# A two-layer hybrid decoder trunk on one core: the order of all instructions from a list scheduler over the recorded program

## The chip, the core and the metric

One core of one Trainium2 chip runs the whole kernel as one program. The metric is device microseconds of an execution; the kernel before has a median of 1129.89 us over 3 runs. Engines are called as in the profile: PE (TensorE matmul), PEld (its weight load), DVE (VectorE), ACT (ScalarE), POOL (GpSimd), SP (SyncE, which issues most loads).

## The reference, cut to what matters

256 tokens of width 1024 pass two layers. In each, three branches mix tokens from the same normalized input: NSA sparse attention, an RWKV-7 recurrence and an S5 diagonal state-space model; a sigmoid gate per channel merges them. Cross-attention to 256 memory tokens and a SwiGLU feed-forward of width 2816 follow. Each sub-layer normalizes its input and its output (RMSNorm).

```python
def layer(x, p):
    h = rmsnorm(x, p.g0)
    z = h @ w_in          # nsa q | k, v (x3) | gates | rwkv | s5 | 3 merge gates of 1024
    y = sum(sigmoid(g_b) * (branch_b(z_b) @ up_b) for b in (nsa, rwkv, s5))
    x = x + rmsnorm(y @ w_merge_out, p.g1)
    x = x + rmsnorm(cross_attention(rmsnorm(x, p.g2), mem), p.g3)
    x = x + rmsnorm(swiglu(rmsnorm(x, p.g4)), p.g5)
```

All of it is fp32.

## The kernel before, in words

Tokens lie in two tiles of 128 rows, x[0] and x[1] (xt in the code), which stay in SBUF. PE multiplies fp32 operands as sums of products of a high and a low part (hi, lo): one main product is three matmuls, high by high, high by low, low by high (mm3, lines L349 to L351). Weights come in 264 units of 128 x 1024 (class Weights): SP loads a unit into one of 3 raw buffers (L315), ACT copies it to its high part wh (L298), and raw minus wh gives the low part wl (L299, in split). This subtraction is done by DVE or POOL in turns that the table ENGS names by stage (W.engs); up to 3 units are ready ahead, and the last TAIL = 2 have buffers of their own.

The main products of a layer run in one stream (mixer_main): q, k and v of NSA, the inputs of RWKV and S5, the merge gates, the products of the branches' outputs (up) and their merge. The branches (rwkv, s5, nsa) are streams of small products, transposes and elementwise work. A stream yields where its next product waits for other engines, and drive steps through the streams by a string, MIX, with one letter a step (m main, r, s, n). S5 treats 8 blocks j of states per layer; each ends with four products into a strip of 32 columns of one bank (L925 to L928), after its scans (L916, L917) and POOL's rotations (L919 to L921).

After the mixer come the merge-out product and a chain that is the same after each sub-layer: Post.half squares and scales a half of a tile's result from PSUM (L444 to L447), Post.end takes 1 / rms by Newton steps on one number per token (rsqrt, L366 to L381) and adds to x (L458); NormT.tile then transposes x (L294) and writes its high and low parts (ACT L416, DVE L417), with which the next products begin. So each token tile passes one such chain between two sub-layers. At the boundary of the layers the last LAST = 4 units of tile 1's feed-forward are held back (finish) and stand behind the first steps of layer 1's q.

The order on each engine is the tile framework's: it takes the program order that streams and drive give, and reorders by its own timeline, with priority to NormT.tile, Post.half and Post.end (decorator first, HPX = 30).

```python
with tile.TileContext(nc, schedule_with_timeline_sim=True) as tc:
    body(tc, t)
```

## Time and profile before

| | before |
|---|---|
| runs, us | 1126.42, 1129.89, 1131.2 (median 1129.89) |
| span of the profiled execution, us | 1125.9; the median of the runs is 4.0 above it (no own time of this execution is listed) |
| busy: PE / PEld / DVE / ACT / POOL | 92% / 80% / 68% / 48% / 57% |
| mean granted TensorE clock | 0.963 |
| moved by DMA | 161.52 MB, mean 143 GB/s |

Busy is a share of the span. Matmuls are pipelined, so a busy PE may still be slower than its pace; the clock says how much of full speed was granted. By stage: start 0 to 28 us, layer 0's mixer 28 to 292, merge-out and cross-attention 292 to 386, feed-forward 386 to 548, boundary of the layers 548 to 591, layer 1's mixer 591 to 844, its cross-attention to 945, feed-forward and end to 1126.

### The profile page before, as it was taken

The page shows a single profiled execution, that of the slowest core. Times are in us where ns is not written, and L with a number is a line of the kernel's source. Part 1 is how long each engine was busy: PE and PEld are TensorE (multiplying, and loading weights), DVE is VectorE, ACT ScalarE, POOL GpSimd, SP SyncE. Part 2 cuts the span into 40 slices and gives each one's busy share as a digit, 9 for nine tenths or more (in the row PEclk, how much of TensorE's full clock was granted, in tenths as well). Part 3 has the DMA queues.
Part 4 walks back from the last instruction along what each step waited for, and adds up shares of the span by engine and source line. Part 5 has one row for each costly group of instructions (what it writes and reads, how often), then busy time and mean ns, then how long its engine had stood idle before and what let it go on. Part 6 is the DMA issues. An engine that isn't in the chain of part 4 may idle for free. (4 is left out here: it accounts for less than half of the span.)

```text
span 1125.9 us, 20473 instructions
## 1 busy us (share of the span) xinstructions
PE 1037.2 (92%) x7890; PEld 900.0 (80%) x7890; DVE 763.2 (68%) x1405; ACT 540.1 (48%) x1040; POOL 647.3 (57%) x762
## 2 busy tenths in 40 slices
PE   8887898999987999999888899999999869999997
PEld 7876676788875799998667776889788748999985
DVE  6667699898766646575458698796995764333633
ACT  7523244456555634454345242545565546444542
POOL 6999787533462586910147578964335434655543
PEclk9998999999988999999989899999899889999999
DMA  6530632244541446555434236223245314655552
GB/s 233 205 122 20 224 115 76 76 155 166 180 141 57 152 159 219 186 185 189 142 100 147 67 113 225 76 93 111 84 164 189 130 56 149 203 183 184 181 192 89
DMA packets 43153, 161.52 MB, mean 143 GB/s; under 512 B 5040, under 2 KB 5168, under 8 KB 41776
## 3 DMA queue, kind: packets, MB, share of 16 engines
q1 hardware_dynamic: 41472, 155.45, 40.7%
q10 hardware_dynamic: 1584, 4.77, 1.2%
q8 instruction: 62, 1.02, 0.4%
q14 instruction: 35, 0.29, 0.1%
HBM read 159.15 MB, written 1.05 MB: 142 GB/s over the span
## 5 line engine op out<-in xcount | busy, mean ns | idle before, releaser
L299 POOL TENSOR_TENSOR wl<-raw,wh 128x1024 fp32r<-128x1024 f32 (+1 forms) x123 | 296.7, 2420 | 327.4 <-ACT wh L298 322.0
L298 ACT ACTIVATE wh<-raw 128x1024 fp32r<-128x1024 f32 (+1 forms) x268 | 282.0, 1055 | 254.5 <-PE mm L350 107.4
L349 PE MATMUL mm<-b,wh 128*128 128x256 f32 x1344 | 386.7, 288 | 2.6 <-DVE b L1274 1.3
L351 PE MATMUL mm<-b,wl 128*128 128x256 f32 x1344 | 386.0, 288 | 1.0 <-DVE wl L299 1.0
L350 PE MATMUL mm<-b,wh 128*128 128x256 f32 x1344 | 384.4, 286 | 0.2 <-DVE b L945 0.2
L299 DVE TENSOR_TENSOR wl<-raw,wh 128x1024 fp32r<-128x1024 f32 (+1 forms) x145 | 196.7, 1357 | 166.8 <-ACT wh L298 166.6
L349 PEld LDWEIGHTS mm<-b,wh 128*128 128x128 f32 x1344 | 256.8, 191 | 12.0 <-issue 4.0
L351 PEld LDWEIGHTS mm<-b,wl 128*128 128x128 f32 x1344 | 256.6, 191 | 9.0 <-issue 6.7
L350 PEld LDWEIGHTS mm<-b,wh 128*128 128x128 f32 x1344 | 256.9, 191 | 5.7 <-issue 4.7
L350 PE MATMUL px<-wl,b 128*128 128x512 f32 x248 | 98.0, 399 | 0.0
L349 PE MATMUL px<-wh,b 128*128 128x512 f32 x248 | 97.0, 401 | 1.0 <-ACT b L298 1.0
L351 PE MATMUL px<-wh,b 128*128 128x512 f32 x248 | 97.2, 400 | 0.0
L349 PE MATMUL mm<-wh,b 128*128 128x512 f32 (+2 forms) x192 | 71.8, 382 | 13.0 <-ACT b L416 8.8
L351 PE MATMUL mm<-wh,b 128*128 128x512 f32 (+2 forms) x192 | 68.5, 370 | 5.5 <-DVE b L417 4.7
L350 PE MATMUL mm<-wl,b 128*128 128x512 f32 (+2 forms) x192 | 68.9, 364 | 0.5 <-DVE wl L299 0.5
L294 PE MATMUL px<-ident,b 128*128 128x128 f32 (+2 forms) x280 | 47.3, 287 | 12.8 <-DVE b L1432 6.7
L349 PEld LDWEIGHTS mm<-wh,b 128*128 128x128 f32 x192 | 39.8, 209 | 22.2 <-ACT b L416 13.4
L349 PEld LDWEIGHTS px<-wh,b 128*128 128x128 f32 x248 | 47.3, 191 | 11.9 <-ACT b L298 1.4
L351 PEld LDWEIGHTS px<-wh,b 128*128 128x128 f32 x248 | 47.1, 190 | 11.2
L350 PEld LDWEIGHTS px<-wl,b 128*128 128x128 f32 x248 | 47.2, 190 | 11.0
L416 ACT ACTIVATE b<-px,cols 128x128 fp32r<-128x128 f32 x128 | 41.1, 366 | 30.1 <-DVE b L417 17.2
L1568 POOL TENSOR_TENSOR b<-b,b 128x256 f32<-128x256 f32 x40 | 39.5, 989 | 26.8 <-ACT b L1567 26.7
(348 smaller groups left out, 1735.7 us busy)
## 6 DMA issues: line engine op xcount, KB each, us to landing
raw<-in_w SPq DMA_DIRECT2D x264, 512.0 KB, 3.5
b<-in_w SPq DMA_DIRECT2D x8, 1024.0 KB, 5.2
b<-in_gains ACTq DMA_DIRECT2D x6, 512.0 KB, 4.1
raw<-in_w SPq DMA_DIRECT2D x6, 420.0 KB, 3.1
b<-in_mem SPq DMA_DIRECT2D x4, 512.0 KB, 5.0
mats<-in_mats SPq DMA_DIRECT2D x1, 1152.0 KB, 7.6
mats<-in_mats ACTq DMA_DIRECT2D x1, 1152.0 KB, 6.8
x<-in_x SPq DMA_DIRECT2D x2, 512.0 KB, 5.3
```

Of the source, the lines that this page charges most:

```text
L294: PE.transpose(out, in_, ident[:k, :k])
L298: A.activation(dst_h, src, AF.Copy)
L299: eng.tensor_tensor(dst_l, src, dst_h.bitcast(F), op=OP.subtract)
L349: PE.matmul(out, lh, rh, start=start, stop=False)
L350: PE.matmul(out, lh, rl, start=False, stop=False)
L351: PE.matmul(out, ll, rh, start=False, stop=stop)
L416: A.activation(self.h[:, n, sl], pt[:, kk], AF.Copy, scale=g[:, n:n + 1])
L1568: G.tensor_tensor(s_, s_, tg[:, 1], op=OP.mult)
```

## The change

The body is run once with engines that only record: each call on DVE, POOL, ACT, PE or SP is kept with its stream (w for weights, m, r, s, n in the mixers, M elsewhere), and all tiles get tags and numbers of buffers. A function plan then lays these operations out in time by a model of costs and takes the order on each engine from it; it also chooses between DVE and POOL for elementwise operations of 64 elements a row or more whose operands all lie in SBUF, between DVE and ACT for plain copies, and among the 8 PSUM banks (tile names bank0 to bank7). The body is run again with these banks, and the operations are issued in that order under a manual schedule, from one line, L2171; so every instruction of the changed kernel has this line. The main products (mm3) keep their order among themselves.

```diff
+class Eng:
...
+            elif what in EITHER and on in (("V",), ("G",)):
...
+                if xs and not any(x.tensor.name in r.psum for x in xs) and _count(xs[0].ap[1:]) >= 64:
+                    on = ("V", "G")
+            r.ops.append((on, what, a, k, r.stream, r.chain))
...
+def _locks(op, eng, out, ins, psum):
+    if eng == "G":
+        return op[1] != "memset"
+    if eng != "V" or any(x.tensor.name in psum for x in out + ins):
+        return False
+    if op[1] in ("tensor_copy", "tensor_scalar"):
+        return _count(out[0].ap[1:]) >= 64 or op[1] == "tensor_copy"
+    return len(ins) > 1
...
+def plan(rec, info=None):
...
+        al = ALPHA.get(ops[i][4], 1.0)
...
+        for j, kind in succ[i] + extra.get(i, []):
+            b = max(b, lvl[j] + ((lat + SEM) if kind else occ) * al)
...
+    for q, bonus in BONUS.items():
...
+            lvl[i] += 1000 * bonus[k * len(bonus) // len(js)]
...
+            if info[j]["locks"].get(e):
+                wait = max(wait, shared)
...
+            if e == "PE":
+                sh, cs = info[j]["cells"]
+                if sh == shape:
+                    wait = max([wait] + [cell[x][y] for x, y in cs])
...
[...]
...
+            if sh != shape:
+                now = max([now] + [x for y in cell for x in y]) + SWITCH
```

BONUS holds, for each stream, 24 numbers of us that are added to the priority of its pieces, and ALPHA a factor on the paths of r, s and n (2.0, 2.2, 2.0). The body itself changes in these places:

```diff
-BUFS = {'tiny': 17, 'b1': 10, 'b2': 20, 'b4': 6, 'b8': 4}
+BUFS = {'tiny': 17, 'b1': 9, 'b2': 21, 'b4': 6, 'b8': 4}
...
-TAIL = 2  # last units of weights, which have buffers of their own
+W_SLOTS = {"raw": 3, "wh": 4, "wl": 4}
...
-            yield
-            o = pyy[q, J]
-            PE.matmul(o, CC[:, 0, j], q1[:, 0], start=True, stop=False)
-            PE.matmul(o, CC[:, 1, j], q1[:, 1], start=False, stop=False)
-            PE.matmul(o, CC[:, 2, j], q2[:, 0], start=False, stop=False)
-            PE.matmul(o, CC[:, 2, j], q2[:, 1], start=False, stop=True)
+            qs.append((pyy[q, J], j, q1, q2))
+            if len(qs) == NB:
+                for n, (c_, i) in enumerate(((0, 0), (1, 1), (2, 0), (2, 1))):
+                    for o, j_, q1, q2 in qs:
+                        PE.matmul(o, CC[:, c_, j_], (q1, q2)[n // 2][:, i], start=n == 0, stop=n == 3)
...
-            for qq in range(2):
-                w1 = sb([P, 2048])
+            for qq in range(4):
+                w1 = sb([P, 1024])
...
-            tc.keep_in_program_order(load_mats(0, m))
+            load_mats(0, m)
...
-        W.engs = engs(2 if l else 1)
...
+    with tc.manual_schedule():
+        for i, e in planned[0]:
...
+            getattr(real[e], what)(*a, **k)
```

MIX loses two letters of its first string; ENGS, W.engs and the decorator first have no effect any more. At the boundary, finish() now stands ahead of taking q's four units in the code. In NormT.tile the two banks of a token tile are evicted in turns. On SP the constants (128 x 1830) and mats (128 x 2304) come ahead of the fourth unit of weights; before, both stood behind the tenth.

Three places of the order follow. The chain of main products is interrupted by other matmuls in 177 places before and in 264 now; DVE has 142 low parts (wl) before and 262 now, POOL 120 and 2.

DVE after layer 0's merge-out: Post's last half, the Newton steps on tiny tiles, the addition to x. Before:

```order
L373 TENSOR_SCALAR tiny_813_3948<-tiny_782_3812 128x1
L445 TENSOR_TENSOR b4_784_3814<-px_780_3810,b4_776_3805 128x512
L366 SCALAR_TENSOR_TENSOR tiny_814_3950<-tiny_813_3948,tiny_782_3812 128x1
L447 TENSOR_SCALAR tiny_785_3815<-tiny_785_3815 128x1
L378 SCALAR_TENSOR_TENSOR tiny_815_3952<-tiny_814_3950 128x1
L379 SCALAR_TENSOR_TENSOR tiny_816_3953<-tiny_815_3952,tiny_813_3948 128x1
L366 SCALAR_TENSOR_TENSOR tiny_818_3957<-tiny_816_3953,tiny_782_3812 128x1
L381 SCALAR_TENSOR_TENSOR tiny_817_3954<-tiny_818_3957,tiny_816_3953 128x1
L373 TENSOR_SCALAR tiny_819_3989<-tiny_785_3815 128x1
L458 SCALAR_TENSOR_TENSOR x_2_81<-b4_781_3811,tiny_817_3954,x_2_81 128x512 x2
```

and now:

```order
L2171 TENSOR_SCALAR tiny_630_704<-tiny_599_673 128x1
L2171 SCALAR_TENSOR_TENSOR tiny_631_705<-tiny_630_704,tiny_599_673 128x1
L2171 SCALAR_TENSOR_TENSOR tiny_632_706<-tiny_631_705 128x1
L2171 SCALAR_TENSOR_TENSOR tiny_633_707<-tiny_632_706,tiny_630_704 128x1
L2171 SCALAR_TENSOR_TENSOR tiny_635_709<-tiny_633_707,tiny_599_673 128x1
L2171 TENSOR_TENSOR wl_647_721<-raw_645_719,wh_646_720 128x1024
L2171 SCALAR_TENSOR_TENSOR tiny_634_708<-tiny_635_709,tiny_633_707 128x1
L2171 SCALAR_TENSOR_TENSOR x_1_74<-b4_598_672,tiny_634_708,x_1_74 128x512
L2171 TENSOR_TENSOR wl_650_724<-raw_648_722,wh_649_723 128x1024
L2171 SCALAR_TENSOR_TENSOR x_1_74<-b4_598_672,tiny_634_708,x_1_74 128x512
L2171 TENSOR_TENSOR wl_663_737<-raw_661_735,wh_662_736 128x1024
L2171 SCALAR_TENSOR_TENSOR b8_562_636<-bank7_71,cols_3_77,b8_561_635 128x128
```

The steps of one token tile now stand together, with one wl among them and two around the addition. Before, those of both tiles alternate, and no wl stands among them on DVE; POOL's own order has a row of wl there.

PE at the boundary of the layers. x_2_81 is the first token tile before, x_1_74 now; px_1274 and bank4_68 hold the second half of tile 1's feed-forward. Before:

```order
L349 MATMUL px_1274_6291<-wh_1350_6640,b2_1356_6664 128x512
L350 MATMUL px_1274_6291<-wl_1351_6641,b2_1356_6664 128x512
L351 MATMUL px_1274_6291<-wh_1350_6640,b2_1357_6665 128x512
L349 MATMUL px_1274_6291<-wh_1353_6658,b2_1356_6664 128x512
L350 MATMUL px_1274_6291<-wl_1354_6659,b2_1356_6664 128x512
L351 MATMUL px_1274_6291<-wh_1353_6658,b2_1357_6665 128x512
L294 MATMUL px_1391_6798<-ident_79,x_2_81 128x128 x4
L294 MATMUL px_1392_6811<-ident_79,x_2_81 128x128 x4
L349 MATMUL mm_1403_6843<-wh_1358_6668,b8_1268_6284 128x512
L350 MATMUL mm_1403_6843<-wl_1359_6669,b8_1268_6284 128x512
```

and now:

```order
L2171 MATMUL bank4_68<-wh_1117_1191,b2_1107_1181 128x512
L2171 MATMUL bank4_68<-wh_1120_1194,b2_1114_1188 128x512
L2171 MATMUL bank4_68<-wl_1121_1195,b2_1114_1188 128x512
L2171 MATMUL bank4_68<-wh_1120_1194,b2_1115_1189 128x512
L2171 MATMUL bank5_69<-ident_73,x_1_74 128x128 x4
L2171 MATMUL bank4_68<-wh_1123_1197,b2_1114_1188 128x512
L2171 MATMUL bank4_68<-wl_1124_1198,b2_1114_1188 128x512
L2171 MATMUL bank4_68<-wh_1123_1197,b2_1115_1189 128x512
L2171 MATMUL bank3_67<-ident_73,x_1_74 128x128 x4
L2171 MATMUL bank1_65<-wh_1138_1212,b8_1030_1104 128x512
```

The transposes of tile 0 (4 each, two banks) stand behind all of tile 1's products before, and now 9 products into its last bank, with three more between them; tile 0's own products end 14 products ahead of them before and 21 now.

PE in layer 0's mixer. Before, single steps of the branches stand between main products (mm_394 is an input of a branch, L677 a step of RWKV, L925 to L928 S5's products, CC their factors):

```order
L349 MATMUL mm_394_1711<-b8_9_95,wh_332_1401 128x256
L350 MATMUL mm_394_1711<-b8_10_96,wh_332_1401 128x256
L351 MATMUL mm_394_1711<-b8_9_95,wl_333_1402 128x256
L349 MATMUL mm_394_1711<-b8_9_95,wh_332_1401 128x256
L677 MATMUL px_336_1427<-b2_225_927,b8_222_906 64x32 x16
L925 MATMUL px_294_1233<-b2_303_1259,CC_176_692 32x256
L926 MATMUL px_294_1233<-b2_303_1259,CC_176_692 32x256
L927 MATMUL px_294_1233<-b2_304_1260,CC_176_692 32x256
L928 MATMUL px_294_1233<-b2_304_1260,CC_176_692 32x256
L294 MATMUL px_346_1474<-ident_79,b1_320_1375 128x128
L294 MATMUL px_346_1474<-ident_79,b1_325_1387 128x128
L925 MATMUL px_294_1233<-b2_343_1468,CC_176_692 32x256
```

Now the main products up to the gates come first, and 451 other matmuls follow with none of them between (in the kernel before the longest such run has 128). Its beginning (ident marks transposes):

```order
L2171 MATMUL bank2_66<-b8_6_80,wh_528_602 128x256
L2171 MATMUL bank2_66<-b8_5_79,wl_529_603 128x256
L2171 MATMUL bank4_68<-b2_188_262,b8_187_261 64x32 x16
L2171 MATMUL bank4_68<-b4_184_258,b2_186_260 64x128 x16
L2171 MATMUL bank4_68<-ident_73,b2_39_113 128x128
L2171 MATMUL bank4_68<-ident_73,b2_41_115 128x128
L2171 MATMUL bank4_68<-ident_73,b2_39_113 128x128
L2171 MATMUL bank4_68<-ident_73,b2_41_115 128x128
L2171 MATMUL bank4_68<-b2_189_263,b2_195_269 64x32 x16
```

and a pair of S5's blocks in it, with the same four factors in turns on two strips:

```order
L2171 MATMUL bank5_69<-b4_301_375,b2_283_357 32x256 x4
L2171 MATMUL bank7_71<-b2_249_323,CC_147_221 32x256
L2171 MATMUL bank7_71<-b2_281_355,CC_147_221 32x256
L2171 MATMUL bank7_71<-b2_249_323,CC_147_221 32x256
L2171 MATMUL bank7_71<-b2_281_355,CC_147_221 32x256
L2171 MATMUL bank7_71<-b2_250_324,CC_147_221 32x256
L2171 MATMUL bank7_71<-b2_282_356,CC_147_221 32x256
L2171 MATMUL bank7_71<-b2_250_324,CC_147_221 32x256
L2171 MATMUL bank7_71<-b2_282_356,CC_147_221 32x256
L2171 MATMUL bank6_70<-ident_73,b1_261_335 128x128
```

What one stream issued before between main products now stands beside the other streams' steps.

## Rows read from the trace of the kernel before

**Rows 1.** The page, part 1: engine, busy us (share of the span), instructions.

```profile
PE 1037.2 (92%) x7890; PEld 900.0 (80%) x7890; DVE 763.2 (68%) x1405; ACT 540.1 (48%) x1040; POOL 647.3 (57%) x762
```

**Rows 2.** Windows: span, length, busy us (instructions) by engine, clock, DMA share, GB/s.

```profile
0.00:28.00 28.00, 24.39 (x135) 20.40 (x136) 17.07 (x49) 19.86 (x37) 17.70 (x48) 1.00 0.67 232
28.00:292.00 264.00, 240.79 (x2176) 202.39 (x2175) 215.28 (x409) 121.11 (x272) 187.74 (x275) 0.97 0.38 130
313.00:386.00 73.00, 58.61 (x352) 48.48 (x351) 51.04 (x139) 40.63 (x97) 31.84 (x21) 0.88 0.30 103
386.00:548.00 162.00, 161.93 (x1154) 151.91 (x1154) 95.40 (x90) 74.14 (x94) 82.23 (x188) 1.00 0.57 191
548.00:591.00 43.00, 34.20 (x161) 27.81 (x160) 24.13 (x63) 20.19 (x42) 17.46 (x9) 0.88 0.30 99
591.00:844.00 253.00, 236.60 (x2138) 199.12 (x2137) 210.87 (x388) 119.04 (x267) 161.82 (x148) 0.97 0.35 120
871.00:945.00 74.00, 59.34 (x347) 48.62 (x346) 48.33 (x138) 40.50 (x96) 29.46 (x14) 0.86 0.28 94
```

**Rows 3.** Windows, PE: two full stretches; then line L349 in both mixers.

```profile
1000.00:1050.00 50.00, 50.00 (x424) 1.00 0.56 184
510.00:545.00 35.00, 35.00 (x152) 1.00 0.57 193
...
28.00:292.00 264.00, 106.41 (x352) 0.97 0.38 130
591.00:844.00 253.00, 102.02 (x339) 0.97 0.35 120
```

**Rows 4.** Windows: the stretch with the longest run of small products.

```profile
79.00:110.00 31.00, 24.38 (x313) 21.03 (x312) 20.69 (x39) 9.93 (x21) 29.41 (x70) 0.83 0.09 29
```

**Rows 5.** Timeline, DVE, boundary: start us, us, engine, line, operation, out<-in.

```profile
558.18 0.16 DVE L378 SCALAR_TENSOR_TENSOR tiny<-tiny 128x1 f32<-128x1 f32 x1
558.38 2.24 DVE L379 SCALAR_TENSOR_TENSOR tiny<-tiny,tiny 128x1 f32<-128x1 f32 x1
560.65 2.26 DVE L366 SCALAR_TENSOR_TENSOR tiny<-tiny,tiny 128x1 f32<-128x1 f32 x1
```

**Rows 6.** Timeline, POOL, the same time.

```profile
558.23 6.97 POOL L299 TENSOR_TENSOR wl<-raw,wh 128x1024 fp32r<-128x1024 f32 x3 [57.78 <-ACT wh L298]
```

**Rows 7.** Timeline, PE, the same time.

```profile
566.05 1.97 PE L294 MATMUL px<-ident,x 128*128 128x128 f32 x8 [6.91 <-DVE x L458]
...
568.67 0.63 PE L351 MATMUL mm<-wh,b 128*128 128x512 f32 x1
569.10 0.63 PE L349 MATMUL mm<-wh,b 128*128 128x512 f32 x1
```

**Rows 8.** Timeline, DVE: ahead of both cross-attentions, and inside one.

```profile
316.19 2.32 DVE L378 SCALAR_TENSOR_TENSOR tiny<-tiny 128x1 f32<-128x1 f32 x1
...
873.74 2.31 DVE L378 SCALAR_TENSOR_TENSOR tiny<-tiny 128x1 f32<-128x1 f32 x1
...
902.56 3.62 DVE L1432 TENSOR_SCALAR b<-b,tiny 128x256 f32<-128x256 f32 x2
```

**Rows 9.** Groups by form (busy us, mean ns); then L299 in 505 to 545.

```profile
L299 POOL TENSOR_TENSOR wl<-raw,wh 128x1024 fp32r<-128x1024 f32 x120 | 290.6, 2429 | 327.2 <-ACT wh L298 321.8 <-DVE b L417 3.3 <-PE px L575 1.8
L299 DVE TENSOR_TENSOR wl<-raw,wh 128x1024 fp32r<-128x1024 f32 x142 | 193.4, 1362 | 164.0 <-ACT wh L298 163.8
...
L1298 DVE TENSOR_TENSOR th<-mm,row 128x256 f32<-128x256 f32 x16 | 6.6, 415 | 0.9 <-PE mm L351 0.9
...
L299 DVE TENSOR_TENSOR wl<-raw,wh x15: 1207/1226/1227, 504.5 to 543.5; 128x1024 fp32r<-128x1024 f32 x15
```

**Rows 10.** Timeline, PE: 32-column strips, of S5 and of the compressed blocks.

```profile
116.43 0.59 PE L927 MATMUL px<-b,CC 128*32 128x256 f32 x2
116.86 0.59 PE L928 MATMUL px<-b,CC 128*32 128x256 f32 x2
...
125.85 1.07 PE L1092 MATMUL px<-b,b 128*32 128x256 f32 x16 [0.99 <-DVE b L1085]
```

More of the change, by code (lines that the diff above doesn't have):

```diff
@@ L1246, in body @@
     W = Weights(order)
-    def engs(n):
-        return [{"V": V, "G": G}[e] for e in ENGS[n]]
     def drive(order, **streams):
@@ L1473, in body @@
     for l in range(L):
-        w = [x_ for u in range(4) for x_ in W.rows(2, 512)]
         if l > 0:
             finish()
+        w = [x_ for u in range(4) for x_ in W.rows(2, 512)]
         enter(nT, 0)
```

629 lines of the change are left out of this document (549 added, 80 removed).

## The prediction, made before the changed kernel ran

> **What bounds the kernel now.** I read the page's busy times first, then a table of the span by stages, then the order of time around the places where TensorE (PE) stands still. The page says that PE is busy 1037.2 of 1125.9 us (92%), and no other engine over 68% [rows 1]. So the span is PE's, and what a new order can give is in the stages where PE is idle or slower than its own pace. The table of stages shows which [rows 2]. The feed-forward stretch of 162 us is full (161.93 busy, granted clock 1.00): nothing is to be had there. The two mixers have 264 us (28 to 292, layer 0) and 253 us (591 to 844, layer 1), the two cross-attention stretches 73 and 74 us with PE busy 58.61 and 59.34 at a clock of 0.88 and 0.86, and the boundary between the layers 43 us with 34.20 busy at 0.88.
>
> Busy time alone hides part of it, since a matmul that waits for its turn or runs at the lower clock counts as busy. So I took PE's pace from two full stretches: 424 products of 256 columns in 50 us are 0.118 us each, 152 of 512 columns in 35 us are 0.230 us [rows 3]. Layer 0's mixer has 3 × 352 = 1056 main products [rows 3]; by the loops of kv_part 48 of them have 512 columns, the others I take as 256: 48 × 0.23 + 1008 × 0.118 = 130 us. The other 134 us of the 264 go to the 2176 - 1056 = 1120 small matmuls of the three branches, 0.120 us each. In a stretch that is nearly all small ones (79 to 110, 51 main products among 313) they take (31 - 51 × 0.118) / 262 = 0.095 us, although the clock there is 0.83 [rows 4]. Layer 1's mixer has 339 on each of the three lines [rows 3], 1017 (125 us by the same working), and 128 us for 1121 others, 0.114 each.
>
> **What the other engines do to PE.** The second thing to see is why the short chains between two stages are long. In the boundary, DVE's operations on one number per partition take 0.16 us, then 2.24 and 2.26 one behind the other [rows 5], and a third like them after that. Over the same time POOL runs three subtractions for the low parts of weights, 6.97 us in a row, 2.32 each [rows 6]. So each of DVE's three small operations stands still until one of POOL's ends. PE waits 6.91 us for the residual that comes out of that chain, and its next products come 0.43 us apart, 512 columns, instead of 0.23 [rows 7]: it pays at the lower of its two levels (1.2 against 2.4 GHz) after the idle time. The same lengths stand in front of both cross-attentions (2.32 and 2.31) and inside one (3.62 for two operations) [rows 8].
>
> **The change, part by part.**
>
> *Subtractions from POOL to DVE.* The order puts 262 of the 264 low parts on DVE; before, 120 took POOL 2.429 us each [rows 9]. On DVE with POOL quiet one takes 1.226 [rows 9], so DVE gets 120 × 1.226 = 147 us more. The products of gates and feed-forward that move along (88 in all: 32, 40 and 16 of 256 columns at lines L1301, L1568 and L1323; one of that size takes DVE 0.415 [rows 9]) add 88 × 0.415 = 37. DVE loses what it stood still for POOL: 142 × (1.362 - 1.226) = 19 us on its own subtractions, and 2.1 us each time that a small operation meets a POOL one. Its load is then at most 763 + 147 + 37 - 19 = 928 us, 86% of the span that I forecast, and nearer 800 where the short operations no longer stand still. This costs nothing as long as DVE keeps ahead of PE; in the mixers that cover is thin, and the third rival is about that.
>
> *The chains between stages.* With POOL free there, each stretched operation falls from some 2.3 to 0.2 us. Boundary: 3 × 2.1 = 6.3. Cross, layer 0: 2 × 2.1 = 4.2, from which one subtraction goes off (1.2), as the order has a wl among the small operations: 3.0. Cross, layer 1: 2 × 2.1 = 4.2, and inside it 3.62 against 2 × 0.415 (the nearest row of 256 columns, [rows 9]), 2.8: 7.0. PE waits less, so fewer products run at 0.43: some 8 per stretch at 0.2 are 1.6 us. What is late next is the evictions of the transposes by ACT and DVE, which come from two banks in turns now; they do not go away. I take 7 for the boundary (21 of tile 1's last products now stand between tile 0's last and the first transposes, 14 before), 6 for layer 0's cross stretch, 8 for layer 1's. The 6 is 3.0 + 1.6 and something for the transposes of the memory, which no longer stand in it. From both sides: a gain of 14 and 15 of the 73 and 74 us is all that PE's idle time there holds; nothing is the other end, if DVE's subtractions stand where POOL's stood.
>
> *S5's products in pairs.* Now four products of one strip of 32 columns follow each other at 0.43 us (two trace instructions each); sixteen of a neighbouring kind, over four strips, take 1.07 us together, 0.067 each [rows 10]. A j has 4 × 0.43 = 1.7 us; with two strips in turns half of it goes, if strips run side by side as in that row: 16 × 0.86 = 14 us over both layers. The lower bound is nothing, if they don't.
>
> *Order inside the mixers.* If small matmuls ran at 0.095 us throughout, layer 0 would lose 1120 × (0.120 - 0.095) = 28 us and layer 1 1121 × (0.114 - 0.095) = 21; with 7 each for the pairs, 35 and 28. But layer 0's new order puts the main products up to the gates first and then 451 small ones with no main product between; the longest such run before had 128. Where small ones wait for evictions, nothing fills. At the rate of 79 to 110 (145 of them by the order in 25 us, 0.17 each) the block lasts 78 us. I take a third of the 35 for layer 0, 12, and half of the 28 for layer 1, 14, where the runs are at most some 110 long and main products stand between. Bounds for layer 0: a gain of 35, a loss of 43 (second rival).
>
> *The start.* The first 28 us move 232 GB/s and hold 24.39 us of PE work [rows 2]. The constants (0.94 MB) and mats (1.18 MB) now come ahead of the fourth unit of q's weights: 2.1 MB at that rate are 9 us. PE has the products of three units for both tiles meanwhile, and what is loaded early is not loaded late. I take a loss of 3; bounds 9 and a gain of 2.
>
> *No cost:* the engines named by turns (ENGS), the three raw buffers, the last two units without buffers of their own, and the compressed blocks' weights in four loads of half the size. The feed-forward has PE at 161.93 of 162, with POOL and DVE under 60% busy. If that cover is gone, a late unit costs PE its 1.2 us.
>
> The sum: + 3 - 12 - 6 - 7 - 14 - 8 = - 44. From the profiled 1125.9 that is 1082; the median of the runs (1129.9) stands 4 above the span, so I forecast 1086.
>
> **The rivals.**
>
> *More than I take (1055).* An order that fills by path length and knows which operations of DVE and POOL block each other may bring layer 1's mixer to PE's pace (28) and layer 0's two thirds of the way (23), and take 10 from each cross stretch: with 7 for the boundary and 3 lost at the start, - 75 from 1126 is 1051, and 4 above it 1055. For it: PE's plain idle time in these stages is 23 + 16 + 14 + 15 + 9 = 77 us [rows 2]. Against it: the chains inside the branches are as long as before.
>
> *The block of small products (1141).* Place: layer 0's mixer, after the gates. There each of the 451 waits for evictions and not only for PE: 0.17 us is their rate with main products near, 0.415 is one eviction of 256 columns from PSUM on DVE [rows 9], which is the rate if every product had to wait for one. Midway, at 0.294, the block takes 133 us instead of 78, 55 more than in the forecast: 1141. It decides from 0.28 on (+ 50, 1136). For it: DVE was busy 215.28 of 264 us in that stage [rows 2] and has more to do now. Against it: three branches stand side by side in the block, not one, and most evictions take several products at once.
>
> *Given back by DVE (1129).* Subtractions and gates from POOL come to a DVE that is busy 215.28 and 210.87 us in the two mixers [rows 2]. If what it no longer stands still for POOL doesn't make up for them, DVE is full there, products wait for low parts, and neither mixer gains (+ 26); the chains give 10 of their 21, with low parts among their operations (+ 11), and the start loses 9 (+ 6): - 44 + 43 = - 1. Then the change moves work and not time, and doesn't do what it says.
>
> *More changes of shape on PE (1110).* Other matmuls interrupt the chain of main products 264 times, 177 before. If all that small matmuls take beyond 0.095 us (28 + 21 us) came from those 177 places, each would cost 0.28, and 87 more 24 us: 1110. Against it: most of the new ones are one or two transposes of the full 128 × 128 tile, the shape of the main products. The Trainium skill speaks for it (TensorEngine Tiling (Array Packing), Tiling Modes, Key Properties): a change of the tiling mode drains the engine, a change of tile within a mode does not. No row here shows such a drain by itself.
>
> **How the numbers follow.** Forecast 0.45, with a range of its own of 1066 to 1108 (the cross stretches and mixers 20 better or worse). More 0.23. Shapes on PE 0.06 (faster too). Given back 0.09. The block 0.17. About 0.5%, 5.6 us, is what a measurement of this kernel can tell from no change (its runs lie 4.8 apart): faster is below 1124.2, slower above 1135.5. Faster: 0.45 + 0.23 + 0.06 = 0.74; same 0.09; slower 0.17. The likeliest case gives 1086. The range goes from 1050, 5 below the better rival, to 1130, which takes in shapes and the case given back; the block lies outside.
>
> **What would show it.** Right: DVE's operations on one number per partition at 0.2 us in all three chains; POOL's busy time under half of 647; DVE at 800 to 930; PE's wait ahead of the boundary's transposes under 2 us, of 6.91; granted clocks above 0.9 in the cross stretches; S5's eight products of a pair in some 1.8 us and not 3.4. Layer 0's mixer should take some 250 us, layer 1's 240. Wrong: small products in layer 0's block over 0.25 us apart, with DVE or ACT as what PE waits for; PE waiting for wl in the mixers; a fourth unit of q that lands 6 us or more after the others' products are done.

## The result, and the profile after

| | before | after |
|---|---|---|
| median of 20 runs, us | 1128.21 (1121.04 to 1133.47) | 1116.26 (1108.84 to 1128.18) |
| ratio, 95% interval | | 0.9876 [0.985, 0.9901] |
| span of the profiled execution, us | 1125.9 | 1107.9 |
| its granted TensorE clock | 0.963 | 0.961 |

The change makes the kernel faster by 1.2%, some 14 us by the ratio; forecast were 44. The profiled execution (1109.84 us) is 18 us shorter than that of before. Nine of the 20 executions of the changed kernel, most of which the ratio leaves out, take 1123 to 1128 us at a mean clock of 0.941 to 0.946.

The page of the changed kernel, part 1 and the clock of part 2 (40 slices, tenths of full speed), to be read against [rows 1]:

```profile
PE 1055.2 (95%) x7890; PEld 900.4 (81%) x7890; DVE 813.8 (73%) x1740; ACT 554.9 (50%) x1079; POOL 168.5 (15%) x388
...
PEclk8999967779999999999999899999999999999999
```

POOL fell from 647.3 to 168.5 us and DVE rose by 51, as the low parts went over. PE has the same 7890 instructions and is busy 18 us longer in a span 18 us shorter: its share rose because its work takes longer, too. The slices of the clock show one place for it, the sixth to the ninth, about 140 to 250 us.

Windows by stage (length, busy us and instructions of PE, PEld, DVE, ACT, POOL, clock, DMA share, GB/s), cut where the stages of the changed kernel lie:

```profile
0.00:28.00 28.00, 21.72 (x94) 18.18 (x95) 16.39 (x49) 17.78 (x35) 15.13 (x56) 0.88 0.63 249
33.00:308.00 275.00, 255.15 (x2161) 211.03 (x2161) 217.12 (x492) 120.97 (x266) 58.69 (x123) 0.88 0.35 114
...
329.00:393.00 64.00, 57.40 (x368) 46.00 (x366) 52.23 (x155) 48.49 (x118) 0.00 (x0) 0.97 0.37 116
393.00:555.00 162.00, 162.00 (x1156) 153.03 (x1155) 114.61 (x167) 73.22 (x91) 51.36 (x149) 1.00 0.63 200
555.00:589.00 34.00, 31.25 (x161) 24.71 (x160) 28.31 (x74) 19.21 (x39) 0.82 (x1) 1.00 0.43 135
589.00:839.00 250.00, 245.44 (x2124) 196.14 (x2123) 185.09 (x416) 119.61 (x269) 36.76 (x42) 0.99 0.37 120
...
865.00:926.00 61.00, 56.03 (x361) 43.92 (x360) 51.45 (x156) 48.25 (x118) 0.76 (x4) 1.00 0.39 121
33.00:144.00 111.00, 110.91 (x854) 103.20 (x853) 90.31 (x178) 58.81 (x94) 39.83 (x95) 1.00 0.53 172
144.00:246.00 102.00, 83.24 (x853) 56.88 (x853) 78.22 (x186) 23.49 (x64) 18.12 (x28) 0.70 0.16 53
```

Beside [rows 2]: the three chains are short (64, 34 and 61 us for 73, 43 and 74) and their clock is up from 0.88, 0.88, 0.86. Layer 0's mixer is longer (275 for 264) at 0.88 for 0.97. The last two windows cut it in two: the main products up to the gates run without a gap, and then the block of 451 small products takes 102 us at 0.70. Stage by stage, from the first main product of a stage to that of the next:

| stage | before, us | after, us | difference | forecast |
|---|---|---|---|---|
| start | 28 | 32.9 | +4.9 | +3 |
| layer 0's mixer | 264 | 274.7 | +10.7 | -12 |
| merge-out, cross-attention | 94 | 85.6 | -8.4 | -6 |
| boundary | 43 | 34.3 | -8.7 | -7 |
| layer 1's mixer | 253 | 249.5 | -3.5 | -14 |
| its cross-attention | 74 | 61.1 | -12.9 | -8 |

The feed-forward and the end did not change. So the chains gave 30 us for 21, and the mixers took 7 where 26 were to be gained.

DVE at the boundary (timeline: start us, us, engine, line, operation, out<-in), the small operations of one token tile, two of which stand in [rows 5], and then PE there:

```profile
562.47 0.14 DVE L2171 TENSOR_SCALAR tiny<-tiny 128x1 int32<-128x1 int32 x1
562.65 0.22 DVE L2171 SCALAR_TENSOR_TENSOR tiny<-tiny,tiny 128x1 f32<-128x1 f32 x1
562.90 0.16 DVE L2171 SCALAR_TENSOR_TENSOR tiny<-tiny 128x1 f32<-128x1 f32 x1
563.10 0.61 DVE L2171 SCALAR_TENSOR_TENSOR tiny<-tiny,tiny 128x1 f32<-128x1 f32 x3
```

```profile
565.35 0.39 PE L2171 MATMUL bank<-wh,b 128*128 128x512 f32 x1
565.58 0.60 PE L2171 MATMUL bank<-ident,x 128*128 128x128 f32 x4
565.93 0.48 PE L2171 MATMUL bank<-wh,b 128*128 128x512 f32 x1
...
569.44 0.73 PE L2171 MATMUL bank<-wh,b 128*128 128x512 f32 x2 [0.70 <-DVE b L2171]
```

None of the small operations is stretched to 2.2 us, the transposes stand between products and wait for nothing (6.91 us before, [rows 7]), and PE's stops at the boundary are all under 1 us: 0.70 for the eviction shown, and the longest, 0.82 at 572.39, for a low part.

PE in layer 0's mixer of the changed kernel: ahead of the block, at its beginning, and where a pair of S5's blocks is done:

```profile
133.52 0.40 PE L2171 MATMUL bank<-b,wh 128*128 128x256 f32 x2
133.76 0.28 PE L2171 MATMUL bank<-b,wl 128*128 128x256 f32 x1
...
134.89 0.43 PE L2171 MATMUL bank<-b,b 64*64 64x128 f32 x4
135.25 0.38 PE L2171 MATMUL bank<-b,wh 128*128 128x256 f32 x1
135.57 0.43 PE L2171 MATMUL bank<-b,b 64*64 64x128 f32 x4
...
136.25 0.43 PE L2171 MATMUL bank<-b,b 64*64 64x128 f32 x4
136.61 0.39 PE L2171 MATMUL bank<-b,wl 128*128 128x256 f32 x1
136.84 0.40 PE L2171 MATMUL bank<-b,wh 128*128 128x256 f32 x2
...
137.55 0.40 PE L2171 MATMUL bank<-b,wh 128*128 128x256 f32 x2
137.88 0.44 PE L2171 MATMUL bank<-b,b 64*64 64x128 f32 x4
...
146.24 1.12 PE L2171 MATMUL bank<-b,b 64*64 64x32 f32 x32 [2.33 <-DVE b L2171]
147.89 1.97 PE L2171 MATMUL bank<-b,b 64*64 64x128 f32 x16 [0.53 <-DVE b L2171]
...
155.22 1.92 PE L2171 MATMUL bank<-b,b 64*64 64x32 f32 x32 [0.69 <-ACT b L2171]
...
223.87 1.94 PE L2171 MATMUL bank<-b,CC 128*32 128x256 f32 x16
```

Two prices stand here that the forecast lacked. The first is a **change of tile shape**: a main product starts 0.12 us after the one before it (133.52 for two, then 133.76), but among 64x64 tiles, at the full clock, the next tiles start 0.32 us after it (135.25, 135.57). Over all 72 places at full clock where a main product of 256 columns stands ahead of 64x64 tiles, and nothing waits, I count 0.21 us in 34 and 0.31 or 0.32 in 38; to its own shape it is 0.12. What stands ahead of the product tells the two apart: in all 34 it is another product of the 128x128 shape, in all 38 it is small tiles, so that the main product stands alone. Going in has a price of its own: the first main product behind 64x64 tiles takes 0.22 us to the second, in 34 of 35 places (136.61 to 136.84). So a change costs 0.10 us on the way in and 0.09 on the way out (137.55 holds two products, the second starts at 137.67, and the tiles follow at 137.88), and a product that stands alone pays both, 0.19. The second is the **clock**: 32 instructions of 64x32 take 1.12 us at 146.24 and 1.92 at 155.22, the lower level. The pair's eight products take 1.94 us; 1.8 were forecast.

To see what each cost, I took every PE instruction of the mixers with the time to the next one, and what its kind needs at full clock among its own shape. What goes beyond it falls under the wait that the trace names, under the lower level where the clock was there, under the change of shape where the next tile has another, or is left over:

| mixer, us | products | waits | changes of shape at full clock (all changes) | lost at the lower level (us spent there) | left over |
|---|---|---|---|---|---|
| layer 0 before | 194.9 | 23.2 | 20.0 (149) | 6.6 (17.1) | 19.3 |
| layer 0 after | 192.3 | 19.8 | 19.5 (208) | 35.3 (64.9) | 7.7 |
| layer 1 before | 189.4 | 16.4 | 19.4 (151) | 7.7 (17.1) | 20.1 |
| layer 1 after | 187.5 | 4.6 | 39.7 (314) | 3.3 (6.8) | 14.4 |

Layer 0 lost 29 us more at the lower level, layer 1 20 us more in changes of shape, twice as many. These tables are my accounts of one execution each; whether they are causes is for the experiments.

### The profile page after: what moved, and what is told of

Its sections match the earlier page's. It is cut to its first block, busy times and chain, and to the rows that moved or that the text cites. A ratio compares the mean times of both kernels' runs of the same rounds, so it can differ in the third digit from the quotient of the medians.

```text
span 1107.9 us, 20410 instructions
## 1 busy us (share of the span) xinstructions
PE 1055.2 (95%) x7890; PEld 900.4 (81%) x7890; DVE 813.8 (73%) x1740; ACT 554.9 (50%) x1079; POOL 168.5 (15%) x388
## 4 chain that ended last, share of the span: by engine, by line
PE 59%; DVE 10%; ACT 6%; issue 1%; DMA 0%; DVEq 0%; ACTq 0%
PE bank L2171 59%; ACT b L2171 4%; DVE b L2171 3%; DVE wl L2171 3%; DVE tiny L2171 2%; ACT wh L2171 2%; DVE x L2171 1%; DVE th L2171 0%; DMA raw<-in_w 0%; DVE bank L2171 0%; DVE rstd L2171 0%; DVEq L2194 0%; ACT L2171 0%; ACT dt L2171 0%; ACTq L2171 0%
## 5 line engine op out<-in xcount | busy, mean ns | idle before, releaser
L2171 PE MATMUL bank<-b,wh 128*128 128x256 f32 x2688 | 514.9, 289 | 3.4 <-DVE b L2171 2.1
L2171 PEld LDWEIGHTS bank<-b,wh 128*128 128x128 f32 x2688 | 425.9, 192 | 17.8 <-issue 7.9
L2171 ACT ACTIVATE wh<-raw 128x1024 fp32r<-128x1024 f32 (+1 forms) x270 | 284.8, 1055 | 294.1 <-PE bank L2171 213.1
L2171 DVE TENSOR_TENSOR wl<-raw,wh 128x1024 fp32r<-128x1024 f32 (+1 forms) x266 | 324.9, 1222 | 113.6 <-ACT wh L2171 110.6
L2171 PE MATMUL bank<-b,wl 128*128 128x256 f32 x1344 | 387.6, 288 | 0.4 <-DVE wl L2171 0.4
L2171 PE MATMUL bank<-wh,b 128*128 128x512 f32 (+2 forms) x896 | 268.0, 377 | 6.8 <-DVE b L2171 4.2
L2171 PEld LDWEIGHTS bank<-b,wl 128*128 128x128 f32 x1344 | 258.2, 192 | 7.0 <-issue 4.1
L2171 PEld LDWEIGHTS bank<-wh,b 128*128 128x128 f32 x896 | 162.5, 189 | 43.9 <-DVE b L2171 10.4
L2171 PE MATMUL bank<-wl,b 128*128 128x512 f32 (+2 forms) x448 | 167.9, 375 | 2.5 <-DVE wl L2171 2.2
L2171 PE MATMUL bank<-b,b 64*64 64x32 f32 (+9 forms) x1696 | 143.5, 282 | 17.0 <-DVE b L2171 9.2
L2171 ACT ACTIVATE b<-bank 128x512 f32<-128x512 f32 (+10 forms) x169 | 76.1, 459 | 143.1 <-PE bank L2171 129.4
L2171 PEld LDWEIGHTS bank<-b,b 64*64 64x64 f32 (+3 forms) x1696 | 90.8, 150 | 63.9 <-issue 18.5
L2171 DVE TENSOR_TENSOR b<-b,b 128x256 f32<-128x256 f32 (+3 forms) x201 | 92.8, 489 | 14.3 <-ACT b L2171 11.1
L2171 PEld LDWEIGHTS bank<-wl,b 128*128 128x128 f32 x448 | 84.9, 189 | 19.5 <-DVE wl L2171 5.4
L2171 DVE TENSOR_TENSOR b<-bank,b 128x512 f32<-128x512 f32 (+3 forms) x102 | 55.8, 566 | 17.3 <-ACT b L2171 10.9
L2171 PE MATMUL bank<-ident,b 128*128 128x128 f32 (+3 forms) x344 | 61.0, 288 | 4.6 <-DVE b L2171 3.0
L2171 ACT ACTIVATE b<-b 128x256 f32<-128x256 f32 (+5 forms) x88 | 45.1, 514 | 28.7 <-DVE b L2171 26.4
L2171 DVE TENSOR_TENSOR b<-bank,row 128x512 f32<-128x512 f32 (+1 forms) x60 | 35.9, 600 | 22.3 <-PE bank L2171 22.2
L2171 PEld LDWEIGHTS bank<-ident,b 128*128 128x128 f32 (+3 forms) x344 | 35.0, 136 | 18.5 <-ACT b L2171 5.6
L2171 POOL TENSOR_TENSOR b<-b,b 128x256 f32<-128x256 f32 (+2 forms) x35 | 29.6, 850 | 123.6 <-DVE b L2171 117.0
L2171 POOL TENSOR_SCALAR tiny<-tiny 128x8 f32<-128x8 f32 x112 | 44.5, 403 | 5.9
L2171 ACT ACTIVATE b<-bank,cols 128x128 fp32r<-128x128 f32 x128 | 39.6, 371 | 9.7 <-DVE b L2171 6.1
```

The costliest lines, as they stand in the source:

```text
L2171: getattr(real[e], what)(*a, **k)
```

## The experiments

**Take the block apart (e1).** Half of each branch gets 100 us more priority, so small products mix with the main products; the plan is made anew.

```diff
-            lvl[i] += 1000 * bonus[k * len(bonus) // len(js)]
+            lvl[i] += 1000 * bonus[k * len(bonus) // len(js)] + 1000 * (100 if q in "rsn" and 2 * k < len(js) else 0)
```

> The branches of layer 0 get 100 us more priority in the list scheduler, so that their small products stand between the main products of the gates and not behind them: the longest run without a main product falls from 451 to 50, and the changes of tile shape on PE in layer 0 rise from some 210 to 470. Theory A (the block cost its time by the lower clock): the time at the lower level in layer 0's mixer falls from 65 us to under 25, and the mixer gets shorter by 20 us or more before what the changes of shape cost. Theory B (each change of tile shape holds PE some 0.1 us): 260 more cost 26 us. Both together leave 1110 to 1122 us; A alone 1096; B alone 1140. Rival C (the chains of the branches over DVE and ACT set the end of the mixer wherever their products stand): the clock recovers and the branches still end at the same time, within 5 us of 1116.

1157.71 us, ratio 1.0264 [1.0217, 1.0312]. PE in the mix, and two windows of it:

```profile
125.76 0.43 PE L2171 MATMUL bank<-b,b 64*64 64x32 f32 x4
126.12 0.58 PE L2171 MATMUL bank<-b,wh 128*128 128x256 f32 x1
126.63 0.43 PE L2171 MATMUL bank<-b,b 64*64 64x32 f32 x4
126.99 0.58 PE L2171 MATMUL bank<-b,wl 128*128 128x256 f32 x1
```

```profile
100.00:164.00 64.00, 64.00 (x384) 43.48 (x384) 28.81 (x69) 10.89 (x20) 11.16 (x15) 0.57 0.28 95
34.00:345.00 311.00, 307.60 (x2148) 229.14 (x2147) 208.03 (x469) 122.11 (x272) 60.12 (x127) 0.85 0.30 99
```

Waits are nearly gone (3.4 us in layer 0's mixer) and that mixer got 36 us longer: 466 changes of shape for 208, and 96 us at the lower level for 65. That a spread block would get the clock back is refuted: PE is busy all 64 of 64 us and the clock is 0.57. The price per change is there, and higher at the lower level: a main product that stands alone starts 0.51 us before the next small tiles (126.12, 126.63), for 0.32 at full clock, and 0.21 before a product of its own shape at this level.

**Keep the block, take out changes (e5).** After the plan, up to 8 main products out of the next 24 PE operations are pulled ahead of a short run of small tiles, as far as inputs, banks and the order of the main chain allow. All other engines keep their order.

```diff
-    return [(i, e) for _, i, e in order], banks, order, info
+    lst = regroup([(i, e) for _, i, e in order], ops, info, rec.psum, banks)
+    return lst, banks, order, info
...
+def regroup(lst, ops, info, psum, banks, W=24, K=8):
...
+        pe = [k for k in range(p, min(len(lst), p + 400)) if lst[k][1] == "PE"][:W]
+        lastsmall = max(k for k in pe if info[lst[k][0]]["cells"][0] != full)
+        mains = [k for k in pe if k < lastsmall and info[lst[k][0]]["cells"][0] == full]
...
+        for k in mains[:K]:
...
+            if bad:
+                break
+            lst.insert(ins, lst.pop(k))
```

> The changed kernel with its order kept on all engines but one: on PE, up to 8 main products that stand between short runs of small tiles are pulled ahead of these runs, so that changes of tile shape fall from 522 to about 340 in the mixers (layer 1 from 314 to some 180); the block of 451 stays. Theory B (a change of shape holds PE some 0.1 us: the spacing after a main product is 0.21 us into another shape and 0.12 without): PE has 17 to 20 us less to do, most of it in layer 1, and the time falls to 1098 to 1104. Rival C (the branches' chains over DVE and ACT end when they end): what PE gains becomes wait, or the clock falls, and the time stays within 4 us of 1116.

1106.75 us, ratio 0.9792 [0.9769, 0.9816]. Changes of shape fall from 208 and 314 to 154 and 176. Layer 1's mixer goes from 249.5 to 245.4: by the account above, 18 us less in changes, 9 more in waits, 6 more at the lower level. Layer 0's keeps its length: pulled main products are done earlier, but the block ends at the same time. So 15 of the 18 us that the changes give in layer 1 come back as waits and at the lower level, and the mixer is 4 us shorter; the rest of the 9.5 us between the medians does not stand in these two profiles.

**Both together (e9).** Regrouping on top of e1's priorities.

> The branches of layer 0 with 100 us more priority, as in e1_spread, and the main products pulled ahead of short runs of small tiles on PE, as in e5_regroup: changes of tile shape in layer 0 fall from 444 to some 230, the longest run without a main product stays at 54. If e1_spread lost its 41 us by the changes of shape (each some 0.1 us at full clock, double at the lower level, and the lower level because of them), layer 0's mixer comes back by 40 us or more and the time is at or below 1107. Theory C goes further: the branches' chains now start some 60 us earlier than in the changed kernel and end earlier, and layer 0's mixer is shorter than there: 1085 to 1100. Rival: small tiles between main products keep the clock low whatever their order, and layer 0's mixer stays 20 us or more behind the changed kernel: above 1125.

1102.99 us, ratio 0.9753 [0.9725, 0.9782], 55 us under e1 with the same priorities. Layer 0's mixer ends at 304 us, for 345 in e1 and 308 in the changed kernel: some 41 us for 237 changes fewer (229 for 466), 0.17 us each, in which the clock gives (44 us at the lower level for 96) and waits take some 10 us. The main products that stand alone in it fall from 125 to 1. Spreading alone loses, regrouping alone gains nothing in layer 0, together they gain. Layer 0's mixer is still not shorter than before the change (269 for 264).

**How far to pull (e10, e13).** e10 is e9 with less priority and longer pulls, e13 is e9 with shorter ones, from a shorter look-ahead (the next 12 PE operations for 24).

```diff
-def regroup(lst, ops, info, psum, banks, W=24, K=8):
+def regroup(lst, ops, info, psum, banks, W=48, K=16):
...
-            lvl[i] += 1000 * bonus[k * len(bonus) // len(js)] + 1000 * (100 if q in "rsn" and 2 * k < len(js) else 0)
+            lvl[i] += 1000 * bonus[k * len(bonus) // len(js)] + 1000 * (70 if q in "rsn" and 2 * k < len(js) else 0)
```

> The same with 70 us more priority instead of 100, and up to 16 main products pulled ahead: some 200 changes of shape in layer 0 and 170 in layer 1. By the same theories: 1085 to 1100 if the chains bound layer 0's mixer and the changes of shape cost as measured, above 1125 if the clock stays low between small tiles. Against e9_spread_regroup it has 35 fewer changes of shape in layer 0, which is worth 3 to 7 us.

1131.7 us, ratio 1.0009 [0.9987, 1.003]: fewest changes of these (186 and 159), but 24 us of waits in each mixer and 51 and 38 us at the lower level. Small products that are held back too long are late for the engines behind them. Priority and length were changed together, so their shares are not told apart.

```diff
-def regroup(lst, ops, info, psum, banks, W=24, K=8):
+def regroup(lst, ops, info, psum, banks, W=12, K=4):
```

> As e9_spread_regroup, but with at most 4 main products pulled ahead at a time instead of 8: some 260 changes of shape in layer 0 and 200 in layer 1 (229 and 176 there). Between e1_spread (none pulled: 444 changes, 3.4 us of waits in layer 0's mixer, 96 us at the lower level) and e10_spread70 (16 pulled: 186 changes, 24 us of waits) it asks where the two prices balance. If a change of shape at 0.1 to 0.2 us is all that counts, 55 more cost 6 to 10 us: 1109 to 1113. If small products that stand later behind pulled main ones turn into waits and these into the lower level, fewer pulled give some of that back: 1098 to 1104.

**1084.22 us, ratio 0.9618 [0.9575, 0.9662]**: 44 us under before, some 30 under the changed kernel, the best version of the study. The page, and windows of both mixers:

```profile
PE 1039.1 (96%) x7890; PEld 891.5 (82%) x7890; DVE 807.4 (75%) x1726; ACT 556.8 (51%) x1084; POOL 173.2 (16%) x397
...
PEclk8999996999999999999999999999999999999999
```

```profile
35.00:294.00 259.00, 251.68 (x2150) 206.59 (x2149) 208.50 (x470) 122.16 (x272) 62.66 (x127) 0.95 0.35 120
576.00:813.00 237.00, 230.72 (x2117) 189.65 (x2116) 184.26 (x415) 119.20 (x269) 36.61 (x42) 0.99 0.39 126
```

The mixers are 259 and 237 us long (275 and 250 in the changed kernel), with 259 and 200 changes, 7.3 and 6.3 us of waits, 27 and 7 us at the lower level. With 4 pulled there are more changes than with 8 (229 and 176) and the time is 19 us shorter: what counts is the sum of changes, waits and clock. The runs show no price that can be taken down by itself.

**Fill the block with work (e6).** 42 products of zeros (128x128, 256 columns) ahead of 25 products that wait in the block, into a bank that is written anew behind them.

```diff
+FILL = {941: 5, 957: 1, 965: 2, 973: 2, 977: 2, 993: 1,
...
+                for _ in range(FILL.get(n_pe, 0)):
+                    nc.tensor.matmul(banks[FILL_BANK][:, 0:256], wz, cst[:, 0:256], start=True, stop=True)
```

> The changed kernel with 42 products of zeros added (128 x 128 tile, 256 columns, 0.43 us each at full clock, into a bank that is free there), in front of those 25 products of layer 0's block ahead of which PE waited 0.3 us or more. Theory A (the block costs by the lower clock, which comes with a PE that has little to do): the time at the lower level in the block falls from 65 to under 35 us, and the block is shorter by 5 to 15 us in spite of 18 us of added products: 1101 to 1111. Rival: the clock stays as it is or the small tiles are what it follows; the added work costs its time, as it doesn't fit into the waits at half speed: 1120 to 1136.

1118.34 us (1105 to 1126), ratio 0.9836 [0.9787, 0.9884]. Windows of its block, and of a stretch of layer 1's mixer:

```profile
144.00:247.00 103.00, 98.29 (x940) 66.02 (x938) 78.67 (x185) 23.55 (x64) 18.67 (x28) 0.82 0.17 52
...
708.00:742.00 34.00, 34.00 (x179) 25.47 (x178) 7.74 (x15) 6.16 (x14) 1.65 (x2) 0.50 0.15 47
```

The clock of the block rises from 0.70 to 0.82 (37 us at the lower level for 61) and PE's idle time in it falls from 19 to 5 us, but its length stays at 102 to 103 us. The filling itself is 18 us of work at full clock (84 instructions, 0.215 us apart) and brings 21 more changes of shape (112 for 91), and it takes what clock and waits give. So whether the lower level alone makes the block long is neither shown nor refuted. The second row is a stretch of layer 1's mixer, whose order is that of the changed kernel: with it, this execution (1125.8 us) has that mixer at 263 us for 250, so its total tells nothing of the block.

**Pairs alone (e4).** The kernel before with S5's products in pairs and nothing else.

```diff
-BUFS = {'tiny': 17, 'b1': 10, 'b2': 20, 'b4': 6, 'b8': 4}
+BUFS = {'tiny': 17, 'b1': 9, 'b2': 21, 'b4': 6, 'b8': 4}
...
+            qs.append((pyy[q, J], j, q1, q2))
+            if len(qs) == NB:
+                for n, (c_, i) in enumerate(((0, 0), (1, 1), (2, 0), (2, 1))):
+                    for o, j_, q1, q2 in qs:
+                        PE.matmul(o, CC[:, c_, j_], (q1, q2)[n // 2][:, i], start=n == 0, stop=n == 3)
```

> The kernel before, with S5's four products of two blocks in turns on two strips (and one 512-element buffer more, one 256-element buffer less, without which it doesn't fit). As priced: PE is less busy by 14 us over both mixers, and the time falls to 1114. Rival: PE waits for other engines in the mixers anyway, and pairs make a strip wait for the second block: 1128, within 4.

1138.4 us, ratio 1.0092 [1.0063, 1.012], slower than before. Its mixers:

```profile
28.00:295.00 267.00, 239.52 (x2179) 206.89 (x2178) 209.82 (x410) 122.15 (x273) 187.79 (x278) 0.92 0.38 128
590.00:851.00 261.00, 235.93 (x2141) 203.49 (x2140) 208.96 (x383) 117.17 (x261) 162.97 (x150) 0.92 0.35 117
```

The pairs are short here too, and PE is busy 239.52 for 240.79 us and 235.93 for 236.60 [rows 2] although its clock fell from 0.97 to 0.92; 82 us of the mixers are at the lower level, for 34. Waits rose by 4 and 9 us. So in this order the time that the pairs take out of PE comes back as waits and as lower clock. The program order moved along with the loop, so a part, or all, of the loss may be order alone. What the pairs are worth in the new order was not tried.

**The lock, confounded (e3).** The lock is what the plan calls it when DVE's operations stand still while POOL subtracts [rows 5, 6]. Every second low part is forced onto POOL, the plan made anew.

```diff
-            rec.either = ("V", "G")
+            rec.either = ("G",) if self.n % 2 else ("V",)
+            rec.force = True
```

> Every second subtraction for the low parts is forced onto POOL, the order being planned anew with that. If POOL's subtractions are what stretched DVE's small operations, the two cross-attention stretches and the boundary of the layers lose the 30 us that they gained against the kernel before, operations on one number per partition take up to 2.3 us again, and the time is 1135 to 1146. Rival: the gain in these stretches came from the order alone (banks in turns, steps of one tile together): they stay within 8 us in all, and the time within 10 of 1116.

1229.58 us, ratio 1.0889 [1.0807, 1.097]. But the planner knows the lock and made another order: between the same main products, the two cross stretches lose 3.3 and 7.2 us and the boundary 10.2, where one small operation takes 2.33 us (at 641.14), but most of the loss is in the mixers (56 and 39 us; 150 to 330 us has a clock of 0.62). This doesn't isolate the lock.

**The lock, in a fixed order (e8).** The changed kernel's order, in which only the 33 low parts planned inside the three chains go to POOL.

```diff
+SPANS = ((314e3, 372e3), (539e3, 566e3), (836e3, 888e3))
...
+    return [(i, "G" if e == "V" and ops[i][4] == "w" and any(a <= t_ < b for a, b in spans) else e) for t_, i, e in lst]
```

> The changed kernel with its order kept, but the low parts that stand near the chains of both cross-attentions and of the boundary are done on POOL and not on DVE (33 of them). If POOL's subtractions stretch the chains, operations on one number per partition take 2 us and more again there, the three stretches lose most of the 30 us that they gained against the kernel before, and the time is 1136 to 1146. Rival (the stretches gained by their new order): they lose under 8 us, and the time is 1116 to 1124.

1142.27 us, ratio 1.0076 [1.0038, 1.0114], 26 us above the changed kernel. DVE and POOL at the boundary:

```profile
577.15 0.71 DVE L2177 SCALAR_TENSOR_TENSOR tiny<-tiny,tiny 128x1 f32<-128x1 f32 x1
577.90 2.30 DVE L2177 SCALAR_TENSOR_TENSOR tiny<-tiny 128x1 f32<-128x1 f32 x1
580.23 2.27 DVE L2177 SCALAR_TENSOR_TENSOR tiny<-tiny,tiny 128x1 f32<-128x1 f32 x1
```

```profile
575.46 7.01 POOL L2177 TENSOR_TENSOR wl<-raw,wh 128x1024 fp32r<-128x1024 f32 x3 [8.16 <-PE bank L2177]
```

The picture of [rows 5, 6] is back: 2.30 and 2.27 us for 0.16, as long as POOL's three subtractions run. The Trainium skill (SBUF — State Buffer, SBUF: two separate sides) calls the pair of ports that DVE and GpSimd share an exclusive lock, and these rows agree. The three stretches lose 3.7, 4.8 and 8.2 us, 17 of the 30 that they had gained; late low parts are not the reason, as PE waits 2.0 us in the whole run for those from POOL. I put the rest of the gain down to the order of the chains, which no run shows by itself. The profiled execution is 32 us longer than that of the changed kernel: beside these 17, 5 are in the block and 11 in layer 1's mixer, which has 31 us at the lower level (720 to 751).

**The start (e2, e11, e12).** e2 lets the loads of x go ahead of constants and mats on SP.

```diff
+    for k, i in zip(at, [x[0], w[0], w[1], x[1], w[2], w[3]] + q["in_mats"] + q["in_consts"]):
+        order[k] = order[k][0], i, "SP"
```

> Only the first eight loads of SP change places: x, two units, x, two units, then mats and the constants, as in the kernel before. If the late x is what the start lost, the first main product comes at some 8 us and not 13.8, and the time falls by 5 to 6 us, to 1111. Rival: the products wait later for what is loaded later (the fourth unit behind its buffer, mats behind that), and the start gives back what it gains: 1116, within 2.

1116.86 us, ratio 0.99 [0.9863, 0.9938]: no difference to the changed kernel. The first main product comes at 14.9 us (13.8 in the changed kernel, 7.5 before), since PE's order has both tiles' transposes ahead of it, whatever lands first. e11 therefore also puts tile 0's evictions ahead of tile 1's and pulls q's first products forward; e12 does the same on e9.

```diff
+    for e_ in "AV":  # the evictions of tile 0 ahead of those of tile 1
...
+    for j in [i for i, e in lst if ops[i][5] and e == "PE"][9:9 + n]:
+        pull(j, lambda i, e: bank(i) & bank(j) or e == "PE" and ops[i][5])
```

> The changed kernel with another order in its first 30 us alone: x first on SP (as in e2_x_first), on ACT and DVE the 8 evictions of tile 0's transposes ahead of tile 1's instead of in turns, and q's first main products on PE as soon as tile 0 is there. If the start's loss is that both tiles must be there before the first product, it comes at some 8 to 10 us and not 13.8, and the time falls by 3 to 6 us, to 1110 to 1113. Rival: the branches' chains set the end of layer 0's mixer and begin no earlier, so the gain is gone by the end of that mixer: 1116, within 2.

> The same in e9_spread_regroup, where PE waits less and the branches begin earlier: 1097 to 1100 if the start counts, 1103 within 2 if not.

1126.16 us, ratio 0.9953 [0.9922, 0.9983], and 1112.78, 0.9881 [0.9862, 0.99]: 9 to 10 us slower than the kernels that they come from. PE in e11:

```profile
10.44 0.79 PE L2205 MATMUL bank<-wh,b 128*128 128x512 f32 x1 [4.46 <-ACT b L2205]
...
24.57 0.49 PE L2205 MATMUL bank<-wh,b 128*128 128x512 f32 x1 [3.59 <-ACT wh L2205]
```

The first product is 3.4 us earlier, but the fourth unit's high part now stands behind tile 1's evictions on ACT, and PE waits 3.59 us for it at 24.57. The products after it run 7 us late, and layer 0's mixer ends 8.6 us later than in the changed kernel: nothing behind a delay at the start takes it up. The edit was misplaced; what a good start would bring stays open.

## Why the prediction was right in its direction and wrong in its size

- **The chains between stages: right, under-sized.** Forecast -21, measured -30. The small operations are at 0.2 us, and the wait ahead of the transposes is gone. e8 shows that the stretched operations cost 17 us there; the forecast had 16 for them (6.3, 3.0 and 7.0). What is left, 13 us, I take for the order, which the forecast under-rated: it let PE's waits for the evictions of the transposes stay, and counted 1.6 us a stretch for products at the lower level, while the clock is now at 0.97 to 1.00.
- **Subtractions from POOL to DVE: right.** Low parts on DVE take 1.22 us for 1.36, DVE has 814 us (800 to 930 expected), POOL 168, and PE waits 2.6 us in all for low parts, 1.2 of them at the boundary. The rival "given back by DVE" doesn't happen.
- **S5's pairs: right in length, not in worth.** 1.94 us a pair for 3.4. The 14 us were counted as if PE's time were the kernel's. In e4, in the old order moved along with the loop, nothing of them is seen: waits and clock took more than they gave.
- **Order inside the mixers: the step that failed.** It forecast -26 and measured +7. It took one rate, 0.095 us for an instruction of a small product (0.17 for a product of the program, which mostly is two of them), from a stretch of before [rows 4], and let it stand for any order. Small products mostly follow their own kind there: I count 13 changes of shape in its 312 instructions, at a clock of 0.83, for 91 in the block's 853, at 0.70, and 314 in some 2120 in layer 1. So the rate holds little of what changes of shape cost (0.09 or 0.10 us each at full clock) and less of the lower level than the block has. The new order has twice as many changes in layer 1 (+20 us) and puts layer 0's small products into a block that runs at 0.70 (+29 us at the lower level in that mixer). Its gain from waits, which the forecast did see, is there: 16.4 to 4.6 us in layer 1. e1 and e9, which differ in PE's order alone, show both prices at work together, and e13, which balances them against waits, comes to 1084, with mixers of 259 and 237 us where the forecast had 250 and 240. How layer 0's loss divides between the two is my account only.
- **The rivals.** Two of them came in part. *Shapes on PE* had 87 more interruptions at 0.28, and an interruption is two changes, in and out; there are 222 more changes of shape in the mixers (522 for 300), since small tiles of different shapes change among each other too, at 0.13 us in the mean of layer 1 (39.7 over 314). So its price was near and its number too low. The Trainium skill's sentence that a change of the tiling mode drains TensorE (TensorEngine Tiling (Array Packing), Key Properties) agrees with the 0.22 us on the way in and the 0.21 on the way out for 0.12. The planner's own price (SWITCH = 95 ns) is what one such change costs at full clock, and stood in the code to be read. *The block* took 102 us, 0.226 a product, midway between the forecast's 0.17 and the 0.28 from which it would have decided; there PE does wait for DVE and ACT (2.33, 0.69 us), as that rival said, and the lower clock is added.
- **The start: nearly right in size (+4.9 for +3), wrong in its reason.** The forecast saw loads; e2 shows that the first products wait for the order of PE, both tiles' transposes first. The fourth unit of q did not become the wait.

What stays open: how long the block would be at the full level (e6 adds work of its own), why the same order in layer 1's mixer runs at the lower level for 31 to 34 us in some executions (e6, e8) and not in that of the changed kernel, how much of e4's loss is program order and what the pairs are worth in the new order.

## What to carry to other kernels

Price a new order of matmuls by what stands next to what: count the changes of tile shape (here 0.09 to 0.10 us each at full clock between main products and 64x64 tiles, so a product alone between small tiles pays for two) and look where the clock goes, since a rate taken from a stretch of before holds only for that stretch's neighbours. Time that is taken out of a busy engine in a stage with waits is not yet time of the kernel; look for what is late next, and sum shapes, waits and clock before calling one of them down. A scheduler's model that knows a price doesn't mean that its order avoids it: here more priority for half of each branch, with a small pass behind the planner that pulls at most four main products forward, was worth some 30 us, and longer pulls (with less priority) lost it all.

## What the runs showed of the hardware that was not expected

- The lower level of the clock comes without any idle time of PE: in e1 PE is busy 64.00 of 64 us with small tiles and single main products in turns, at 0.57; in e6's profile 34.00 of 34 us at 0.50, and 18.00 of 18 us before them, at 1.00. What the two stretches share is small tiles among one to five main products, so many changes of shape. That doesn't decide it: in the profile of the changed kernel the same order in layer 1 runs at 1.00 (700 to 740 us, PE busy 40.00 of 40).
- Less work on PE went with less clock: in e4, with the pairs and the order that they brought along, the mixers went from 0.97 to 0.92.
- A change between main products of 256 columns and 64x64 tiles has a price on both sides at full clock: the first product behind the tiles takes 0.22 us to the next, the last one 0.21 us to the tiles, for 0.12 between others, and one alone 0.31 (38 of 38 places in the changed kernel). At the lower level, in e1, they are 0.38, 0.34 and 0.51 us for 0.21: 0.17 in, 0.13 out, 0.30 for one alone.
